# The opening of a one-core hybrid decoder layer: order of the first loads, norms and splits

## The chip, the cores and the metric

The kernel runs on one core of one Trainium2 chip. The metric is the device time of one execution in microseconds; runs of a kernel are given as their median. A profile is one execution, recorded instruction by instruction. Its engines are TensorE (PE, with its weight loads as PEld), VectorE (DVE), ScalarE (ACT), GpSimd (POOL) and SyncE (SP), which here only issues transfers.

## What is computed

One layer of a hybrid decoder over 512 tokens of width 1024, all in float32:

```
u    = RMSNorm(x) * attn_pre_norm
proj = u @ w_in             # delta-rule q, k, v, gate, beta, decay; attention q, k, v
mix  = concat(gated delta rule(proj), block attention(proj)) @ w_out
h    = x + RMSNorm(mix)
h    = h + RMSNorm(relu(RMSNorm(h) @ w_up)^2 @ w_down)
out  = h + sigmoid(h @ w_ple_gate) * (p @ w_ple)
```

The opening, where the change lies, computes `p @ w_ple` (the embedding, 512 x 256 by 256 x 1024), which is stored to memory (`ple`) and read at the very end, the first RMSNorm and its transposes, and the operands of the first projection.

## The kernel before

PE multiplies in a form (fp32r) that takes one pass; to keep float32 accuracy each operand is split into a high and a low half, and each product is three matmuls (`mm3`, L182 for the first, L185 for the others). A split is a cast on ACT (high) and a subtraction on DVE (low): `part_of` (L223, L224) in the embedding, `load_w` (L160, L161) for weights that are loaded into one of three `raw` buffers, and `put_split` (L197, L198) behind the transposes.

The opening is, in the program's order: loads of p, of w_ple's four quarters (on ACT's queue), of x's first 128 tokens and of the identity; a tile `warm` of zeros (memset on DVE) and three products of zeros on PE (L131); a one-column Square on ACT (L132), the first that needs ACT's table, in place on `warm`; the splits of p and w_ple; `embed(0)`, 24 matmuls of 512 columns for the first 512 columns of the embedding, with four copies out of PSUM and their stores; the splits of the other half of w_ple; the load of the norm's weights `nw0` (128 rows of 4 KB, L243, on ACT's queue); the loads and splits of wv in four quarters, with x's other tiles among them; small constants. Then, for each of four tiles of 128 tokens: a Square with its sum on ACT (L258), the inverse root on POOL (`rsqrt`, L148 and L149), the scaling on DVE (L261), eight transposes on PE (L206), and the split of their result into `uT`. `embed(1)` stands behind the first tile. Then come the wv products, 192 matmuls of 260 columns.

No engine's order is written by hand. A planner takes the program's order as ranks, reckons when each instruction's inputs are there, and from it fixes an order for each engine when the kernel is built. On the chip each engine and each transfer queue follows that order, and waits where an input is late. Names with the same tag share a fixed number of buffers: a new tile waits until an old one was read for the last time. The transfers of SP's and ACT's queues count on eight semaphores in turn.

Of the kernel before, what the change touches and what calls it, by code (L numbers as in the profile page):

```python
# [9 lines left out]
F32 = mybir.dt.float32  # L10
F32R = mybir.dt.float32r
AF = mybir.ActivationFunctionType
# [3 lines left out]
P = 128  # L16
T = 512
NT = T // P
D = 1024
# [49 lines left out]
def hybrid_layer(ctx: ExitStack, tc: tile.TileContext, x, p, w_in, w_tok, w_out, w_up, w_down, w_ple, w_gate,  # L69
                 norms, small, consts, rot, out):  # L70
    nc = tc.nc
    PS = bass.MemoryType.PSUM
    cp = ctx.enter_context(tc.tile_pool(name="cp", bufs=1))
    act = ctx.enter_context(tc.tile_pool(name="act", bufs=1))
    phA = ExitStack()
    wp = phA.enter_context(tc.tile_pool(name="wp", bufs=1, side="right"))
# [18 lines left out]
    def pany(name):  # L95
        turn_no[0] += 1
        return (pmm, plv, pmo)[turn_no[0] % 3](name)
# [14 lines left out]
    kc = actB.tile([P, K_END - P], F32, name="kc")  # L112
    sm = cp.tile([P, 57], F32, name="sm")
    nw0 = e.tile([P, D], F32, name="nw0")
    x_h = [e.tile([P, D], F32, tag="x", bufs=4, name=f"x{t}") for t in range(NT)]
    load_x = lambda t: nc.sync.dma_start(x_h[t], x[t * P:(t + 1) * P, :])
# [6 lines left out]
    nc.sync.dma_start(ident, consts[:, K_ID:K_ID + P])  # L123
    for k in range(2):
        nc.scalar.dma_start(wl_in[:, k, 512:D], w_ple[k * P:(k + 1) * P, 512:D])

    warm = e.tile([P, 512], F32, name="warm")
    nc.vector.memset(warm, 0.0)
    pw = ps.tile([P, 512], F32, tag="tr", bufs=2, name="pwarm")
    for _ in range(3):  # L130
        nc.tensor.matmul(pw, warm[:, :P], warm, start=True, stop=True)  # L131
    nc.scalar.activation(warm[:, 0:1], warm[:, 0:1], AF.Square)  # L132

    kcol = lambda c: kc[:, c - P:c]
    tri, ones, neg, ngt = (kcol(c) for c in (K_TRI, K_ONE, K_NEG, K_NGT))
# [10 lines left out]
    def rsqrt(dst, ss, scale, n, eps=EPS):  # L146

        nc.gpsimd.tensor_scalar(dst, ss, scale, eps, op0=ALU.mult, op1=ALU.add)  # L148
        nc.gpsimd.tensor_tensor(dst, dst, half[:, :n], op=ALU.pow)  # L149


    def load_w(src, k0, nk, cols, name):
        n = nk * cols
        raw = wp.tile([P, 1040], F32, tag="raw", bufs=3, name=f"{name}_r")
        hi = wp.tile([P, 1040], F32R, tag="hi", bufs=4, name=f"{name}_h")
        lo = wp.tile([P, 1040], F32R, tag="lo", bufs=4, name=f"{name}_l")

        nc.sync.dma_start(raw[:, :n].rearrange("p (k c) -> p k c", k=nk),
                          src if len(src.shape) == 3 else src[k0 * P:(k0 + nk) * P, :].rearrange("(k p) c -> p k c", p=P))
        nc.scalar.copy(hi[:, :n], raw[:, :n])  # L160
        nc.vector.tensor_sub(lo[:, :n], raw[:, :n], hi[:, :n].bitcast(F32))  # L161
        return (hi[:, :n].rearrange("p (k c) -> p k c", k=nk), lo[:, :n].rearrange("p (k c) -> p k c", k=nk))

    def load_chunk(src, cols, name, nk=KT):

        per = min(nk, 1024 // cols if cols <= 512 else 2)
        got = []
        for k0 in range(0, nk, per):
            hi, lo = load_w(src, k0, per, cols, f"{name}_{k0}")
            got += [(hi[:, i, :], lo[:, i, :]) for i in range(per)]  # L170
        return got

    def load_rows(src, name, order):
        got = {}
        for k0 in order:
            hi, lo = load_w(src, k0, 2, 512, f"{name}_{k0}")
            for i in range(2):
                got[k0 + i] = (hi[:, i, :], lo[:, i, :])
        return got

    def mm3(dst, l, r, start, stop, w_right=False):
        nc.tensor.matmul(dst, l[0], r[0], start=start, stop=False)  # L182
        ops = [(l[0], r[1]), (l[1], r[0])]
        for i, (a, b) in enumerate(ops[::-1] if w_right else ops):
            nc.tensor.matmul(dst, a, b, start=False, stop=stop and i == 1)  # L185
# [14 lines left out]
    def transpose_in(u, dst, t, name):  # L200

        for q in range(2):
            pt = ptr(f"{name}{t}_{q}")
            for i in range(4):
                k = 4 * q + i
                nc.tensor.transpose(pt[:, i * P:(i + 1) * P], u[:, k * P:(k + 1) * P], ident)  # L206
            s = (slice(None), slice(4 * q, 4 * q + 4), slice(t * P, (t + 1) * P))
            put_split((dst[0][s], dst[1][s]), j4(pt))
# [6 lines left out]
    tk = lambda t: slice(t * P, (t + 1) * P)  # L215
    ple = dr.tile([2, T, 512], F32, name="ple")
# [5 lines left out]
    def part_of(both, src, s):  # L222
        nc.scalar.copy(both[0][s], src[s])  # L223
        nc.vector.tensor_sub(both[1][s], src[s], both[0][s].bitcast(F32))  # L224
# [5 lines left out]
    def embed(i):  # L230
        pts = [pany(f"pl{i}_{t}") for t in range(NT)]
        for k in range(2):
            for t in range(NT):
                mm3(pts[t], (pT[0][:, k, tk(t)], pT[1][:, k, tk(t)]), (wl[0][:, k, hf(i)], wl[1][:, k, hf(i)]),
                    k == 0, k == 1, True)
        for t in range(NT):
            s = e.tile([P, 512], F32, tag="pl", bufs=8, name=f"pls{i}_{t}")
            (nc.vector.tensor_copy if t == 3 else nc.scalar.copy)(s, pts[t])
            nc.sync.dma_start(ple[i, tk(t), :], s)
    embed(0)  # L240
    for k in range(2):
        part_of(wl, wl_in, (slice(None), k, slice(512, D)))
    nc.scalar.dma_start(nw0, norms[0:1, :].to_broadcast([P, D]))  # L243
    wv = []
    for t in range(NT):
        wv += load_chunk(w_tok[t * 256:(t + 1) * 256, :], 520, f"wv{t}", nk=2)
        if t == 0:
            load_x(1)
        if t == 1:
            load_x(2)  # L250
            load_x(3)
    nc.sync.dma_start(sm, small)
    nc.sync.dma_start(kc, consts[:, P:])

    for t in range(NT):
        ss = e.tile([P, 1], F32, tag="s1", bufs=4, name=f"ss{t}")
        u = e.tile([P, D], F32, tag="u", bufs=2, name=f"u{t}")
        nc.scalar.activation(u, x_h[t], AF.Square, accum_out=ss)  # L258
        r = e.tile([P, 1], F32, tag="r1", bufs=4, name=f"r{t}")
        rsqrt(r, ss, 1.0 / D, 1)  # L260
        nc.vector.scalar_tensor_tensor(u, x_h[t], r, nw0, op0=ALU.mult, op1=ALU.mult)  # L261
        transpose_in(u, uT, t, "ut")
        if t == 0:
            embed(1)
    ph1.close()
    g = ph2.enter_context(tc.tile_pool(name="g", bufs=1, reuse_waits="tile"))

# [5 lines left out]
    for t0 in (0, 2):  # L273
        pts = {(t, a): pany(f"wv{t}_{a}") for t in (t0, t0 + 1) for a in (0, 260)}
# [155 lines left out]
    for i in (1, 0):  # L430
        for b in range(4):
            s = slice(b * BLK, (b + 1) * BLK)
# [261 lines left out]
    pts = [pany(f"po0{t}") for t in range(NT)]  # L694
# [102 lines left out]
    for g in range(NS):  # L797
        f = F[g % 2]
# [103 lines left out]
    for i in range(2):  # L902
        sr.give(*(s for p_ in wd_s[4 * i:4 * i + 4] for s in p_))
        wg = [x_ for k0 in range(0, KT, 2) for x_ in halves(load_split(w_gate[:, hf(i)], k0))]
        for t in range(NT):
            for c0, c1 in ((0, 512),) if (i, t) != (1, NT - 1) else ((0, 256), (256, 512)):
                n = c1 - c0
                cs = slice(i * 512 + c0, i * 512 + c1)
                sl = take()
                pl, s = sl[:, 0:512], sl[:, 512:D]  # L910
# [54 lines left out]
```

## Time and profile before

| | |
|---|---|
| runs, median (lowest to highest) | 699.1 us (697.05 to 699.86), n = 3 |
| the profiled execution, its own time | 700.27 us |
| its span, first to last instruction | 698.4 us |
| mean granted clock of PE | 0.996 of 2.4 GHz |
| busy: PE, PEld, DVE, ACT, POOL | 682.5, 564.8, 439.0, 324.5, 48.6 us |

The span leaves out some 1.9 us around the instructions. A busy time is a sum over the whole span; an engine whose share is near 1 leaves little for the others to win, and what a stage is worth is read from the wait that ends last in it. Matmul ends are modelled, so two matmuls in a row overlap in the rows and their starts tell the pace.

### The profile page before, as it was taken

To read this page: it belongs to the slowest core of one execution; us is meant where nothing else is said; L and a number is where in the kernel's file an instruction comes from. 1 tells how busy PE (TensorE), PEld (TensorE's weight loads), DVE (VectorE), ACT (ScalarE), POOL (GpSimd) and SP (SyncE) were. 2 spreads that over 40 slices of the span, in tenths; PEclk is the share of its full clock that TensorE was granted. 3 is DMA by queue.
4 is the path that set the end of the run, shared out by engine and by line. 5 is a ranking of instruction groups with operands and counts; after the bars stand their busy time and mean duration, and the time that the engine had idled before them with its cause. 6 is when DMAs were issued, how large, how long until landed. Compare 5 with 4: busy or idle time off the path is not lost. (4 is left out here: it accounts for less than half of the span.)

```text
span 698.4 us, 9002 instructions
## 1 busy us (share of the span) xinstructions
PE 682.5 (98%) x3418; PEld 564.8 (81%) x3418; DVE 439.0 (63%) x687; ACT 324.5 (46%) x598; POOL 48.6 (7%) x91
## 2 busy tenths in 40 slices
PE   8999999999999999999999999999999999999897
PEld 5998888888877768789888888888888888678786
DVE  4748889367676655675386456955778756634532
ACT  6536343433466655445265644454335454523311
POOL 1401100000011100230000000000000000032100
PEclk9999999999999999999999999999999999999999
DMA  8732323532102028286004440154211124544421
GB/s 331 301 122 61 101 86 105 114 109 92 31 31 61 31 61 309 112 258 255 31 31 150 122 150 31 61 151 151 90 35 56 61 76 136 184 84 121 122 77 47
DMA packets 38556, 79.24 MB, mean 113 GB/s; under 512 B 9776, under 2 KB 10416, under 8 KB 38512
## 3 DMA queue, kind: packets, MB, share of 16 engines
q1 hardware_dynamic: 36640, 74.98, 32.7%
q0 software_dynamic: 1152, 2.10, 1.9%
q10 hardware_dynamic: 720, 1.57, 0.6%
q8 instruction: 27, 0.44, 0.3%
q14 instruction: 17, 0.14, 0.1%
HBM read 70.51 MB, written 7.08 MB: 111 GB/s over the span
## 5 line engine op out<-in xcount | busy, mean ns | idle before, releaser
L185 PE MATMUL pd<-sr,sr 128*128 128x512 f32 x464 | 143.6, 390 | 0.6 <-DVE sr L676 0.5
L185 PE MATMUL pu<-u2Tl,sr 128*128 128x512 f32 (+1 forms) x288 | 105.4, 366 | 0.7 <-DVE u2Tl L198 0.7
L182 PE MATMUL pu<-u2Th,sr 128*128 128x512 f32 (+1 forms) x288 | 105.4, 366 | 0.0
L185 PE MATMUL pu<-u2Th,sr 128*128 128x512 f32 (+1 forms) x288 | 105.2, 365 | 0.0
L185 PEld LDWEIGHTS pd<-sr,sr 128*128 128x128 f32 x464 | 86.9, 188 | 19.8 <-DVE sr L676 1.7
L182 PE MATMUL pd<-sr,sr 128*128 128x512 f32 x232 | 90.7, 391 | 0.5 <-ACT sr L675 0.5
L676 DVE TENSOR_TENSOR sr<-sf,sr 128x1024 fp32r<-128x1024 f32 x48 | 58.6, 1222 | 38.5 <-ACT sr L675 14.9
L676 DVE TENSOR_TENSOR sr<-wd,sr 128x1024 fp32r<-128x1024 f32 x42 | 51.3, 1222 | 29.6 <-PE pu L185 28.1
L770 ACT ACTIVATE f<-pu 128x512 f32<-128x512 f32 (+1 forms) x36 | 19.9, 552 | 95.7 <-PE pu L185 95.7
L675 ACT CAST sr<-sf 128x1024 fp32r<-128x1024 f32 x48 | 50.3, 1047 | 27.3 <-DMA sf<-in_w_ple_gate 11.9
L185 PEld LDWEIGHTS pu<-u2Tl,sr 128*128 128x128 f32 x288 | 54.3, 189 | 9.7 <-DVE u2Tl L198 0.9
L185 PEld LDWEIGHTS pu<-u2Th,sr 128*128 128x128 f32 x288 | 54.3, 189 | 8.8
L182 PEld LDWEIGHTS pu<-u2Th,sr 128*128 128x128 f32 x288 | 54.3, 189 | 8.6
L675 ACT CAST sr<-wd 128x1024 fp32r<-128x1024 f32 x42 | 44.2, 1051 | 19.4 <-PE pd L185 19.4
L182 PEld LDWEIGHTS pd<-sr,sr 128*128 128x128 f32 x232 | 43.6, 188 | 10.1 <-ACT sr L675 1.4
L182 PE MATMUL pc<-uTh,w_h 128*128 128x512 f32 x96 | 39.3, 409 | 0.0
L185 PE MATMUL pc<-uTh,w_l 128*128 128x512 f32 x96 | 38.6, 402 | 0.0
L185 PE MATMUL pc<-uTl,w_h 128*128 128x512 f32 x96 | 38.5, 401 | 0.0
L825 DVE TENSOR_TENSOR sf<-sf,pd 128x512 f32<-128x512 f32 x28 | 19.1, 685 | 22.2 <-PE pd L185 22.2
L830 DVE TENSOR_TENSOR wd<-wd,wd 128x1024 f32<-128x1024 f32 x24 | 29.3, 1223 | 0.6
L182 PE MATMUL pg<-sr,h2Th 128*128 128x512 f32 (+1 forms) x72 | 27.2, 377 | 0.0
L185 PE MATMUL pg<-sr,h2Th 128*128 128x512 f32 (+1 forms) x72 | 27.0, 376 | 0.0
(421 smaller groups left out, 1324.2 us busy)
## 6 DMA issues: line engine op xcount, KB each, us to landing
sf<-in_w_up SPq DMA_DIRECT2D x32, 512.0 KB, 3.3
wd<-in_w_down SPq DMA_DIRECT2D x24, 512.0 KB, 4.7
w_r<-in_w_in SPq DMA_DIRECT2D x12, 512.0 KB, 3.6
wo_r<-in_w_out SPq DMA_DIRECT2D x8, 512.0 KB, 3.7
sf<-in_w_ple_gate SPq DMA_DIRECT2D x8, 512.0 KB, 4.3
sf<-in_w_down SPq DMA_DIRECT2D x8, 512.0 KB, 4.3
wv_r<-in_w_tok SPq DMA_DIRECT2D x4, 520.0 KB, 6.6
x<-in_x SPq DMA_DIRECT2D x4, 512.0 KB, 6.9
```

The costliest lines, as they stand in the source:

```text
L182: nc.tensor.matmul(dst, l[0], r[0], start=start, stop=False)
L185: nc.tensor.matmul(dst, a, b, start=False, stop=stop and i == 1)
L675: nc.scalar.copy(hi, src)
L676: nc.vector.tensor_sub(lo, src, hi.bitcast(F32))
L770: nc.scalar.activation(fq[:, side, c0:c1], pt[:, :n], AF.Relu)
L825: add(dst, dst, pts[j])
L830: sub(B[dst + (kk,)], B[x_ + (kk,)], B[y_ + (kk,)])
```

## The change

- The norm's weights `nw0` are loaded on ACT's queue right after w_ple, and x's second tile on SP's right after the identity.
- Two products of zeros instead of three.
- The one-column Square works on a tile of its own, `first`, which POOL sets to zero.
- `load_w` is cut into `load_raw` (the transfer) and `split_raw` (the cast and the subtraction). wv's first three quarters are loaded before x's third and fourth tile; the fourth after the first is split.
- The embedding's copies alternate between ACT and DVE (before: the fourth on DVE); its stores are issued in one row behind the small constants.
- Ranks: norm 0, `embed(1)`, norm 1, the split of wv's first quarter, loads and stores, the splits of the second and third quarter, norm 2, the split of the fourth, norm 3. Before, all wv splits came ahead of all norms.

```diff
--- before.py
+++ after.py
@@ -123,13 +123,17 @@
     nc.sync.dma_start(ident, consts[:, K_ID:K_ID + P])
     for k in range(2):
         nc.scalar.dma_start(wl_in[:, k, 512:D], w_ple[k * P:(k + 1) * P, 512:D])
+    nc.scalar.dma_start(nw0, norms[0:1, :].to_broadcast([P, D]))
+    load_x(1)
 
     warm = e.tile([P, 512], F32, name="warm")
     nc.vector.memset(warm, 0.0)
     pw = ps.tile([P, 512], F32, tag="tr", bufs=2, name="pwarm")
-    for _ in range(3):
+    for _ in range(2):
         nc.tensor.matmul(pw, warm[:, :P], warm, start=True, stop=True)
-    nc.scalar.activation(warm[:, 0:1], warm[:, 0:1], AF.Square)
+    first = cp.tile([P, 1], F32, name="first")
+    nc.gpsimd.memset(first, 0.0)
+    nc.scalar.activation(first, first, AF.Square)
 
     kcol = lambda c: kc[:, c - P:c]
     tri, ones, neg, ngt = (kcol(c) for c in (K_TRI, K_ONE, K_NEG, K_NGT))
@@ -149,17 +153,23 @@
         nc.gpsimd.tensor_tensor(dst, dst, half[:, :n], op=ALU.pow)
 
 
-    def load_w(src, k0, nk, cols, name):
+    def load_raw(src, k0, nk, cols, name):
+        raw = wp.tile([P, 1040], F32, tag="raw", bufs=3, name=f"{name}_r")
+
+        nc.sync.dma_start(raw[:, :nk * cols].rearrange("p (k c) -> p k c", k=nk),
+                          src if len(src.shape) == 3 else src[k0 * P:(k0 + nk) * P, :].rearrange("(k p) c -> p k c", p=P))
+        return raw
+
+    def split_raw(raw, nk, cols, name):
         n = nk * cols
-        raw = wp.tile([P, 1040], F32, tag="raw", bufs=3, name=f"{name}_r")
         hi = wp.tile([P, 1040], F32R, tag="hi", bufs=4, name=f"{name}_h")
         lo = wp.tile([P, 1040], F32R, tag="lo", bufs=4, name=f"{name}_l")
-
-        nc.sync.dma_start(raw[:, :n].rearrange("p (k c) -> p k c", k=nk),
-                          src if len(src.shape) == 3 else src[k0 * P:(k0 + nk) * P, :].rearrange("(k p) c -> p k c", p=P))
         nc.scalar.copy(hi[:, :n], raw[:, :n])
         nc.vector.tensor_sub(lo[:, :n], raw[:, :n], hi[:, :n].bitcast(F32))
         return (hi[:, :n].rearrange("p (k c) -> p k c", k=nk), lo[:, :n].rearrange("p (k c) -> p k c", k=nk))
+
+    def load_w(src, k0, nk, cols, name):
+        return split_raw(load_raw(src, k0, nk, cols, name), nk, cols, name)
 
     def load_chunk(src, cols, name, nk=KT):
 
@@ -235,24 +245,17 @@
                     k == 0, k == 1, True)
         for t in range(NT):
             s = e.tile([P, 512], F32, tag="pl", bufs=8, name=f"pls{i}_{t}")
-            (nc.vector.tensor_copy if t == 3 else nc.scalar.copy)(s, pts[t])
-            nc.sync.dma_start(ple[i, tk(t), :], s)
+            (nc.scalar.copy, nc.vector.tensor_copy)[t % 2](s, pts[t])
+            pls.append((i, t, s))
+    pls = []
     embed(0)
     for k in range(2):
         part_of(wl, wl_in, (slice(None), k, slice(512, D)))
-    nc.scalar.dma_start(nw0, norms[0:1, :].to_broadcast([P, D]))
-    wv = []
-    for t in range(NT):
-        wv += load_chunk(w_tok[t * 256:(t + 1) * 256, :], 520, f"wv{t}", nk=2)
-        if t == 0:
-            load_x(1)
-        if t == 1:
-            load_x(2)
-            load_x(3)
-    nc.sync.dma_start(sm, small)
-    nc.sync.dma_start(kc, consts[:, P:])
-
-    for t in range(NT):
+    raw_v = [load_raw(w_tok, 2 * i, 2, 520, f"wv{i}") for i in range(3)]
+    load_x(2)
+    load_x(3)
+
+    def norm_in(t):
         ss = e.tile([P, 1], F32, tag="s1", bufs=4, name=f"ss{t}")
         u = e.tile([P, D], F32, tag="u", bufs=2, name=f"u{t}")
         nc.scalar.activation(u, x_h[t], AF.Square, accum_out=ss)
@@ -260,8 +263,25 @@
         rsqrt(r, ss, 1.0 / D, 1)
         nc.vector.scalar_tensor_tensor(u, x_h[t], r, nw0, op0=ALU.mult, op1=ALU.mult)
         transpose_in(u, uT, t, "ut")
-        if t == 0:
-            embed(1)
+    wv = []
+
+    def split_v(i):
+        hi, lo = split_raw(raw_v[i], 2, 520, f"wv{i}")
+        wv.extend((hi[:, j, :], lo[:, j, :]) for j in range(2))
+    norm_in(0)
+    embed(1)
+    norm_in(1)
+    split_v(0)
+    raw_v.append(load_raw(w_tok, 6, 2, 520, "wv3"))
+    nc.sync.dma_start(sm, small)
+    nc.sync.dma_start(kc, consts[:, P:])
+    for i, t, s in pls:
+        nc.sync.dma_start(ple[i, tk(t), :], s)
+    for i in (1, 2):
+        split_v(i)
+    norm_in(2)
+    split_v(3)
+    norm_in(3)
     ph1.close()
     g = ph2.enter_context(tc.tile_pool(name="g", bufs=1, reuse_waits="tile"))
```

## Rows read from the trace of the kernel before

**Rows 1.** The page, its first line and part 1.
```profile
span 698.4 us, 9002 instructions
...
PE 682.5 (98%) x3418; PEld 564.8 (81%) x3418; DVE 439.0 (63%) x687; ACT 324.5 (46%) x598; POOL 48.6 (7%) x91
```

**Rows 2.** Waits of PE, whole run: total us, times, longest us.
```profile
PE ut L206 <- DVE u L261: 0.9, 1, 0.9
...
PE ut L206 <- DVE uTl L198: 0.6, 2, 0.4
```

**Rows 3.** Timeline, PE and weight loads (PEld): start us, length us.
```profile
1.44 5.49 PE L131 MATMUL pwarm<-warm 128*128 128x512 f32 x6 [1.44 <-DVE warm L128]
...
4.17 0.34 PEld L131 LDWEIGHTS pwarm<-warm 128*128 128x128 f32 x1 [0.52 <-issue]
...
5.02 0.34 PEld L131 LDWEIGHTS pwarm<-warm 128*128 128x128 f32 x1 [0.52 <-issue]
...
6.73 0.34 PEld L185 LDWEIGHTS pl<-wlh,pTl 128*128 128x128 f32 x1 [0.52 <-issue]
...
7.16 0.45 PE L185 MATMUL pl<-wlh,pTl 128*128 128x512 f32 x1
...
7.45 0.40 PE L182 MATMUL pl<-wlh,pTh 128*128 128x512 f32 x1
...
7.68 0.39 PE L185 MATMUL pl<-wlh,pTl 128*128 128x512 f32 x1
```

**Rows 4.** Timeline, ACT and its queue, the opening.
```profile
2.62 1.28 ACT L223 ACT_TABLE_LOAD   x1 [2.62 <-issue]
4.09 0.62 ACT L223 CAST pTh<-p_in 128x512 fp32r<-128x512 f32 x1 [0.19 <-DMA p_in<-in_p]
4.62 0.61 ACT L223 CAST wlh<-wl_in 128x512 fp32r<-128x512 f32 x1
6.97 0.20 ACT L132 ACTIVATE warm<-warm 128x1 f32<-128x1 f32 x1 [1.74 <-PE pwarm L131]
7.08 0.60 ACT L223 CAST pTh<-p_in 128x512 fp32r<-128x512 f32 x1
...
9.54 0.62 ACT L223 CAST wlh<-wl_in 128x512 fp32r<-128x512 f32 x1 [0.24 <-DMA wl_in<-in_w_ple]
9.55 0.33 ACTq L243 DMA_DIRECT2D nw<-in_norms  x1
...
14.41 1.05 ACT L258 ACTIVATE u<-x 128x1024 f32<-128x1024 f32 x1
```

**Rows 5.** Timeline, SP's queue, the opening.
```profile
0.73 0.85 SPq L120 DMA_DIRECT2D p_in<-in_p  x2
...
2.10 0.43 SPq L123 DMA_DIRECT2D ident<-in_consts  x1
4.26 0.38 SPq L158 DMA_DIRECT2D wv_r<-in_w_tok  x1
```

**Rows 6.** Landing times: nw0's issue (median), and L121's (min/median/max).
```profile
nw<-in_norms ACTq DMA_DIRECT2D x1, 512.0 KB, 6.6
...
DMA to landing us min/median/max: 3.5/4.4/5.3
```

**Rows 7.** Windows: us, busy (x) of PE, PEld, DVE, ACT, POOL; PEclk, DMA, GB/s.
```profile
7.30:10.70 3.40, 3.40 (x17) 2.80 (x16) 2.49 (x4) 2.24 (x5) 0.00 (x0) 1.00 1.06 405
...
655.00:658.70 3.70, 1.64 (x10) 0.96 (x8) 1.69 (x3) 1.18 (x2) 0.00 (x0) 1.00 0.80 168
658.70:662.60 3.90, 3.90 (x13) 3.12 (x14) 0.98 (x2) 0.59 (x1) 0.00 (x0) 0.57 0.66 192
```

**Rows 8.** Timeline, all engines, around the first norm.
```profile
15.91 0.56 POOL L149 TENSOR_TENSOR r<-r,half 128x1 f32<-128x1 f32 x1
...
16.51 1.28 DVE L261 SCALAR_TENSOR_TENSOR u<-x,r,nw 128x1024 f32<-128x1024 f32 x1 [0.73 <-DMA ple<-pls]
...
17.85 1.09 PE L206 MATMUL ut<-ident,u 128*128 128x128 f32 x8 [0.94 <-DVE u L261]
```

## The prediction

> **What bounds the kernel now.** I read the page's first part, then who TensorE (PE) waited for over the whole run, then the opening engine by engine in order of time. PE is busy 682.5 of 698.4 us [rows 1], and what is left is scattered: of its waits the largest that belong to the opening are 1.4 us before the first product of zeros [rows 3], 0.9 us for u, and 0.6 us (two waits) for the low half of uT [rows 2]. The kernel is bound by PE's work, so the opening is worth what it shifts PE's real work, and everything behind moves with it. The most that can be won is small: the three products of zeros and the waits for u and uT. Against a median of 699.1 us, 0.5% is 3.5 us; the three timed runs lie 2.8 us apart, so less than about that can't be told from no change.
>
> In PE's rows the reader should see steps, since the ends are modelled. The weight loads of the zero products stand 0.85 us apart (4.17, 5.02); there are six, two to a product, the first (counted back) at 1.61, so a product takes 1.71 us and the third ends at 6.73, where the second weight load of the embedding appears [rows 3]. The first two matmuls of the embedding are 0.43 us apart (6.73 to 7.16), later ones 0.23 (7.45 to 7.68): 512 columns at 1.2 and at 2.4 GHz. So the clock rose at about 7.3 us, 5.7 us after the first product began, with PE busy all that time [rows 3].
>
> ACT's rows tell why the embedding could not have waited less. After its four transfer issues ACT loads its table (1.28 us), makes the first high halves at 4.09 and 4.62, and is then stuck until 6.97, because the one-column Square writes the tile that the zero products read; the second half's splits start at 7.08 [rows 4].
>
> **The change part by part.**
>
> *One product less.* The zero products end at 1.61 + 4 x 0.855 = 5.03 instead of 6.73: 1.71 us taken off PE. It is a gain only if the embedding's first operands are there. With the splits where they are now (second cast ends at 4.62 + 0.61 = 5.23 [rows 4]) PE could start at about 5.3.
>
> *The table tile of its own.* The Square no longer waits for PE, so the 1.74 us stall of ACT goes [rows 4]. The new memset is one column on POOL, idle then; POOL's work on norms comes far later [rows 8]. By itself this pulls the second half's splits from 7.08 to about 6.3. PE needs them only after the first 12 matmuls, so it is worth nothing as long as those 12 last longer.
>
> *nw0 on ACT's queue, ahead of the Square and of all splits.* This is the part I think decides. Before, eight transfers are issued at once, four by each queue. SP's last of them is at 2.10; its next one, free of any data dependence, is issued only at 4.26 [rows 5], which is when the first transfer of all has landed (the first issues are at 0.73 [rows 5], the quickest landing takes 3.5 us [rows 6]). So the ninth transfer waits for the first. After the change nw0 follows the four w_ple loads on ACT, and it and x1 are the ninth and tenth. A wait at the head of ACT's queue holds everything behind it on ACT: table load, Square, all six splits; DVE waits for those splits, and PE for both.
>
> Where the planner puts nw0 is not certain. In the trace it deviates from the program's order only for what is not ready: the old Square (program order ahead of the splits) stands behind two of them, and nw0 stands where the program has it, behind the last split [rows 4]. An issue that is ready by the planner's reckoning goes by its place in the program. I take it that nw0 stands right behind the w_ple loads, and the first ACT instruction that needs a table, now the Square, behind nw0.
>
> Then: nw0 waits until 4.26, its issue takes 0.33 to 0.45 us (0.33 for nw0 before [rows 4], 0.43 for SP's issues [rows 5]), so 4.66; table load 1.28, so 5.94; Square, and the first cast 0.11 behind its start as at 6.97 and 7.08, so about 6.1; the second cast 0.53 later, ending at 7.2. PE starts the embedding at about 7.3 instead of 6.73. It has stood idle from 5.03, some 2.3 us.
>
> What a table load costs is weighed once more. Its row is 1.28 us, and the cast behind it started 0.19 us after it ended, with its data just landed [rows 4]. The Trainium skill (ScalarE: Activation LUTs, What ACT_TABLE_LOAD costs) adds a drain of 1.38 us to a load of 1.28. By that the splits would begin 1.4 us later still and PE at 8.7; the trace can't rule out a part of it, since nothing was ready sooner, but a cast 0.19 us behind the load excludes the whole, so I go by the row.
>
> *The clock.* Before, it rose with PE busy from 1.6 to 7.3. With a 2.3 us hole in that stretch I expect it to rise later. Near the end, a stretch of 3.7 us in which PE was busy for 1.64 was followed by one at a mean of 0.57 of full speed, that is, mostly at 1.2 GHz [rows 7]. Bounds, counted in embedding matmuls (0.427 us at 1.2, 0.227 at 2.4): if the clock rises at 7.3 all the same, PE has done by then 1.3 or so fewer, or 0.33 us. If it takes the same 5.66 us from the restart, it rises at 12.96: until then 5.66 / 0.427 = 13.3 matmuls, where before 1.2 + 5.70 / 0.227 = 26.3 were done; 13.1 fewer, or 2.97 us. If it stays low for as long as in that late stretch (a mean of 0.57 over 3.9 us is 3.35 us at half speed), 8.3 fewer, or 1.9 us. I take 2.4, midway between the two latter.
>
> The Trainium skill (TensorE: Matmul & The Clock Gate, What's actually happening) says that the low clock is the default and that only activity releases it. This trace agrees for the start (zero products at half speed). It is the rule that speaks against dropping a product when nothing is ready to take its place.
>
> *Norms ahead of wv's splits, nw0 and x1 early.* Now u of the first tile starts at 16.51, right behind the rsqrt on POOL (15.91 + 0.56 = 16.47), and that hangs on ACT's Square at 14.41, which stood behind a wv split; nw0 landed at 9.55 + 6.6 = 16.15 [rows 4, 6, 8]. So nw0 alone would have won only 0.3 us: ranking the norms is the larger half. After: the last w_ple quarter lands at about 9.5 as now [rows 4]; x1 and nw0, 0.5 MiB each, share 405 GB/s [rows 7] and land near 12.1. ACT squares x0 at about 10.2 (behind the last split), r is there by 12.3, u takes 1.28 us [rows 8], so PE can transpose from 13.6 instead of 17.85. At that time PE is still in the embedding, which lasts until 17 now and to about 19 then: the 0.94 us wait goes. The 0.6 us of waits for uT are for space that the DVE halves free; I take half of them gone. Together -1.2 us (bounds 0 and -1.5 [rows 2]).
>
> *The rest.* wv's loads ahead of x2 and x3: x2 and x3 land one or two transfers later (0.5 MiB at 405 GB/s is 1.3 us each [rows 7]); wv's last quarter waits for a free raw buffer. The ple stores go behind wv's last load, sm and kc: their readers come at the very end, so nothing waits. One more of four ple copies on DVE, under PE's embedding work. Each is covered by PE's own work at that time, embedding or wv products, which in the trace waits only for what is named above [rows 2]; without that cover a late tile or split would cost about a load, 1.3 us. Bounds 0 and +1.
>
> **Sum**: +2.4 (late and cold start) -1.2 (waits for u and uT) = +1.2 us. The profiled execution took 700.27 us, 1.2 above the median of the runs; the sum on the median is 700.3.
>
> **Rivals.**
>
> *A. The Square and table load slip ahead of nw0's wait* (the planner counts nw0 as not ready until a transfer lands, and takes what is). For it: ACT would be idle there, and the planner did move the old Square past what was ready. Against: nw0's own place before. The casts start at 4.1 to 4.7, PE at 5.3 to 5.9, its hole is 0.3 to 0.9 us, and if the clock rises at 7.3 as now PE is 0.4 to 0.75 us ahead by then. With the waits, -0.6 - 1.2 = about -1.8: 697.3 us. If the hole costs the rise after all, about -0.2.
>
> *B. The change of the norms gains nothing*: PE's queue has the first transposes at a fixed place, and if that is planned ahead of the second embedding, PE stalls for u at some 12 to 13.6. Worth +1.2 against my sum, 701.5 us. Against it: the cold start delays PE to about 15 before it gets there.
>
> *C. Slower beyond doubt: the clock stays low well past 13 us.* Each further us at 1.2 GHz costs about half a us. From +1.2 with the rise at about 11.8, +3.5 is reached with the rise at about 16.4. The late stretch, back up after 3.4 us, speaks against it; a hole again at the transposes would speak for it. Say 704 us.
>
> **Chances.** My forecast 0.50, A 0.28, B 0.14, C 0.08. The same cases, with the spread of a median of such runs, give faster by over 0.5% 0.04 (A with a downstream order that happens to suit), within 0.5% 0.86, slower 0.10 (C, and the end of B). The range leaves out C and the outer end of A: from A's 697.3, a little under for the spread of runs, to the upper bound 2.97 with nothing recovered, 702.1. So 697.0 to 702.1; the forecast's own range is 699 to 701.5.
>
> **What would show it.** Right: in ACT's rows nw0's issue at about 4.3 and the table load behind it at 4.7, the first cast near 6.1; PE idle from 5.0 to 7.3; steps of 0.43 us in the embedding past 9 us; no wait for u before the first transposes. Wrong: the table load at 2.6 or 3.1 and casts at 4.1 to 4.7 (A); PE waiting for u at 12 (B). The prediction falls as a whole if the planner's order changes further on, where PE's queue has other waits (the score and transposing stages), since a shift of 2 us there is as large as all that I add up.

## The result and the profile after

The changed kernel takes 705.05 us (703.76 to 706.82, 6 runs), the kernel before, run beside it, 699.48 us (697.05 to 701.78, 6 runs): a ratio of 1.0080, 95% interval 1.0056 to 1.0103. It is 5.6 us slower, above the range that was given (697.0 to 702.1).

The page of the changed kernel, first line and part 1, which answers to [rows 1]:

```profile
span 702.2 us, 8998 instructions
...
PE 685.5 (98%) x3416; PEld 563.9 (80%) x3416; DVE 439.2 (63%) x689; ACT 323.1 (46%) x596; POOL 49.6 (7%) x92
```

PE has one product less to do (two of its rows), and is busy 3.0 us longer. A late start would show as idle time; the longer work has another source, of which a low clock in the opening is at most a part. The opening on ACT and its queue, against [rows 4]:

```profile
4.24 0.33 ACTq L126 DMA_DIRECT2D nw<-in_norms  x1
4.61 1.28 ACT L136 ACT_TABLE_LOAD   x1 [4.61 <-DMA wl_in<-in_w_ple]
5.90 0.20 ACT L136 ACTIVATE first<-first 128x1 f32<-128x1 f32 x1
6.01 0.60 ACT L233 CAST pTh<-p_in 128x512 fp32r<-128x512 f32 x1
...
10.25 1.05 ACT L261 ACTIVATE u<-x 128x1024 f32<-128x1024 f32 x1
```

And on PE, against [rows 3]:

```profile
1.45 3.39 PE L133 MATMUL pwarm<-warm 128*128 128x512 f32 x4 [1.45 <-DVE warm L130]
7.18 0.50 PE L192 MATMUL pl<-wlh,pTh 128*128 128x512 f32 x1 [2.34 <-ACT wlh L233]
7.51 0.43 PE L195 MATMUL pl<-wlh,pTl 128*128 128x512 f32 x1
7.75 0.63 PE L192 MATMUL pl<-wlh,pTh 128*128 128x512 f32 x1
8.17 0.63 PE L195 MATMUL pl<-wlh,pTl 128*128 128x512 f32 x1
...
11.16 0.39 PE L195 MATMUL pl<-wlh,pTl 128*128 128x512 f32 x1
11.38 0.39 PE L195 MATMUL pl<-wll,pTh 128*128 128x512 f32 x1
...
14.38 1.03 PE L216 MATMUL ut<-ident,u 128*128 128x128 f32 x8
```

The scaling on DVE, and windows with the granted clock (the third number from the end):

```profile
12.35 1.28 DVE L264 SCALAR_TENSOR_TENSOR u<-x,r,nw 128x1024 f32<-128x1024 f32 x1 [1.29 <-POOL r L153]
```

```profile
5.00:10.00 5.00, 2.82 (x8) 2.27 (x9) 3.19 (x5) 4.05 (x8) 0.00 (x0) 0.77 1.02 382
10.00:15.00 5.00, 5.00 (x24) 4.07 (x23) 3.22 (x4) 4.77 (x9) 2.13 (x4) 0.89 1.04 410
```

The reader sees nw0's issue at 4.24, the table load behind it, the first cast at 6.01, a hole of 2.34 us on PE, a step of 0.24 (7.51 to 7.75), steps of 0.43 us (7.75 to 8.17) that go on until about 11, then steps of 0.22, and the first transposes at 14.38 with no wait. That is nearly the opening that was forecast (where it differs stands below). What it cost is read where it ends, at the first 512-column product of the projection (`pc`): 47.45 us, before 46.62. So 0.8 us of 5.6.

For the rest I laid the two traces side by side, instruction by instruction. From 45 us on every engine has its instructions in the same order in both, and the same PE instruction starts later and later: by 0.8 us at 45 us, 1.8 at 200, 2.8 at 425, 4.8 at 590. (At the end it is 3.8: waits for transfers differ, and the profiled run of before lost time at a low clock near 660 us [rows 7], which that of after did not.) A drift without a new wait is a matter of pace. PE in the middle of the up projection (`pu`), first before, then after:

```profile
429.90 0.39 PE L185 MATMUL pu<-u2Th,sr 128*128 128x512 f32 x1
430.13 0.39 PE L182 MATMUL pu<-u2Th,sr 128*128 128x512 f32 x1
430.36 0.39 PE L185 MATMUL pu<-u2Tl,sr 128*128 128x512 f32 x1
430.58 0.39 PE L185 MATMUL pu<-u2Th,sr 128*128 128x512 f32 x1
```

```profile
433.73 0.40 PE L192 MATMUL pu<-u2Th,sr 128*128 128x512 f32 x1
433.96 0.39 PE L195 MATMUL pu<-u2Tl,sr 128*128 128x512 f32 x1
434.19 0.40 PE L195 MATMUL pu<-u2Th,sr 128*128 128x512 f32 x1
434.43 0.39 PE L192 MATMUL pu<-u2Th,sr 128*128 128x512 f32 x1
```

Three steps take 0.68 us before and 0.70 after. Over the whole trace, of the steps between 222 and 242 ns (512 columns at 2.4 GHz; 226.7 ns is the mean for `pu` before), 498 of 2253 lie over 229 ns before and 1372 of 2260 after. Their sum over 226.7 ns apiece, called the excess below, is 3.3 us before and 9.3 after. Up to 600 us the two differ by 4.35 us; the drift behind the opening is 4.8 - 0.8 = 4.0.

What differs is where the tiles lie. `first` is one column in the pool `cp`, and the built program gives it 32 bytes of each partition; the tiles that are laid out behind it on that side of memory (uT, the second uT, the first eleven weight slabs `sr`) move up by 32, those at the other end stay. Byte address in the partition, and its remainder modulo 256, of what is streamed and of the weights of the same product, in three products of the built programs:

```
                  streamed, mod 256      weights, mod 256
before  pu   44000 224  u2Tl        142816 224  sr (slab 10)
before  pu   27616 224  u2Th        199136 224  sr (slab 11)
before  pd  208864 224  sr          138720 224  sr (slab 9)
after   pu   44032   0  u2Tl        142848   0  sr (slab 10)
after   pu   27648   0  u2Th        199136 224  sr (slab 11)
after   pd  208864 224  sr          138752   0  sr (slab 9)
```

Sorting the steps by whether the streamed address and that of the next product's weights (PEld loads them meanwhile) are equal modulo 256:

```
              before                         after
            steps  mean ns  over 229 ns   steps  mean ns  over 229 ns
equal        1725   227.05       6%        1056   228.19      24%
not equal     481   231.65      74%        1154   233.16      93%
```

Sorted by the product's own weights the shares come out the same (24% and 93% in the changed kernel), so the traces do not tell which of the two counts. Of the 256 slow steps among the equal ones in the changed kernel, 139 stand right behind an unequal step; behind an equal one only 13% are slow.

### The profile page after: what moved, and what is told of

It reads as the page before. It is cut to its first block, busy times and chain, and to the rows that moved or that the text cites. A ratio compares the mean times of both kernels' runs of the same rounds, so it can differ in the third digit from the quotient of the medians.

```text
span 702.2 us, 8998 instructions
## 1 busy us (share of the span) xinstructions
PE 685.5 (98%) x3416; PEld 563.9 (80%) x3416; DVE 439.2 (63%) x689; ACT 323.1 (46%) x596; POOL 49.6 (7%) x92
## 4 chain that ended last, share of the span: by engine, by line
PE 84%; DMA 7%; DVE 3%; ACT 2%; issue 2%; POOL 1%; ACTq 0%; POOLq 0%; DVEq 0%
PE pu L195 16%; PE pd L195 12%; PE pu L192 8%; PE pc L195 6%; PE pd L192 6%; PE pg L195 3%; PE pc L192 3%; PE po L195 3%; PE pmq L195 2%; PE pmk L195 2%; PE wv L195 2%; DMA sf<-in_w_ple_gate 2%; DMA sf<-hd 2%; PE pz L195 2%; PE pg L192 2%
```

## The experiments

The theories: **place** (the 32 bytes make the later products slow, the opening costs 1 to 2 us), and **opening** (the late start and the cold clock cost it all, and what drifts later is chance). In all runs the table gives the median (number of runs), the ratio to the kernel before run beside it with its 95% interval, the excess, and the start of the first `pc`.

| | us (n) | ratio | excess, us | first `pc`, us |
|---|---|---|---|---|
| before (beside the changed kernel) | 699.48 (6) | 1 | 3.3 | 46.6 |
| after | 705.05 (6) | 1.0080 [1.0056, 1.0103] | 9.3 | 47.5 |
| first_in_e | 701.43 (10) | 1.0028 [1.0013, 1.0043] | 3.3 | 48.6 |
| before_pad32 | 704.13 (7) | 1.0066 [1.0040, 1.0091] | 9.2 | 46.5 |
| before_pad128 | 701.37 (10) | 1.0034 [1.0013, 1.0055] | 7.6 | 46.7 |
| before_pad256 | 699.72 (10) | 1.0002 [0.9981, 1.0022] | 3.3 | 47.3 |
| before_aligned | 698.49 (10) | 0.9987 [0.9963, 1.0011] | 1.3 | 46.5 |
| after_three | 704.97 (4) | 1.0066 [1.0048, 1.0084] | 9.2 | 47.2 |
| open_nw_sp | 700.03 (10) | 1.0013 [0.9994, 1.0032] | 3.4 | 48.5 |
| open_aligned | 700.17 (10) | 0.9995 [0.9976, 1.0013] | 1.3 | 48.3 |
| before_two | 701.00 (11) | 1.0003 [0.9987, 1.0020] | 3.3 | 47.3 |
| before_nw_early | 703.81 (5) | 1.0051 [1.0032, 1.0069] | 3.4 | 51.0 |
| open_nw_late | 704.52 (5) | 1.0063 [1.0038, 1.0089] | 3.3 | 51.9 |
| open_mid | 700.27 (12) | 1.0015 [0.9999, 1.0031] | 1.4 | 49.2 |

One caution for the last column: before_pad256 differs from before in no instruction of PE's opening, and its first `pc` starts 0.7 us later (PE waited 1.9 us for u there, not 0.9, and behind that its granted clock was 0.75 from 20 to 25 us, where before it was 1.00). So in the opening less than about 0.7 us may be chance.

### The place of the tiles

**first_in_e**: the changed kernel, the new tile in the opening's own pool, which lies elsewhere.

```diff
-    first = cp.tile([P, 1], F32, name="first")
+    first = e.tile([P, 1], F32, name="first")
```

> The changed kernel, with the tile first taken from the opening's own pool, so that every later tile lies where it lay before; the opening is as in the changed kernel. Theory P (place): most of the loss is that first moves uT, the norm's slabs and all else on the left side by 32 bytes, and a 512-column product goes at 0.233 us instead of 0.227 where streamed operand and next weights no longer lie at equal addresses modulo 256. Then the pace is that of before (some 500 of 2250 steps slow, about 3.3 us over 226.7 ns in all) and only the opening's 0.8 us stays: about 700.3 on a before of 699.5 (699 to 701.5). Rival O (opening: the late and cold start and what follows from it): stays near 705. Rival I (PE's instruction stream is two products shorter and falls differently into its fetches): stays near 705.

The excess is back at 3.3 us and the drift is gone: against before, PE is 2.0 us late from 50 us to 600 us. What is left of the change, a ratio of 1.0028, is its opening.

**before_pad32**, and the same with 32 and 64 columns (**before_pad128**, **before_pad256**): the kernel before with a tile that nothing uses, ahead of the others.

```diff
+    pad = cp.tile([P, 1], F32, name="pad")
+    nc.gpsimd.memset(pad[:, 0:1], 0.0)
     half = cp.tile([P, 16], F32, name="half")
```

> The kernel before, with a one-column tile (32 bytes of each partition) put ahead of the tile half and one POOL memset on it; nothing else. Theory P: all of the loss of pace without the change of the opening: some 1400 slow steps of 2250, about 9.3 us over 226.7 ns, 6 us more than before: about 705 (704 to 706.5). Rivals O and I: no change, 699.5 within 1.

> The kernel before, with a tile of 64 columns (256 bytes) at the same place. Theory P with the period of 256 bytes that the two traces show: no change of pace (500 slow steps), 699.5 within 1. A rival form of P (any move of the left side against the right, or a boundary of 512 or 1024 bytes) would give slow steps and up to 6 us more. Rivals O and I: no change.

> The kernel before with 128 bytes ahead of the tile half. Theory P with a period of 256 bytes: 1133 pairs unequal instead of 578, but unequal by 128 where they were equal, and those are slow in 8 of 10 cases in the two traces: 5 us over before, about 703.5 to 705. With a period of 128 or 64 bytes: no change, 699.5.

The opening of before, untouched, and yet 4.6 us slower with 32 bytes (1.0066), and nothing with 256. PE in `pu` in the two kernels, 32 bytes first:

```profile
429.71 0.39 PE L187 MATMUL pu<-u2Th,sr 128*128 128x512 f32 x1
429.95 0.40 PE L184 MATMUL pu<-u2Th,sr 128*128 128x512 f32 x1
430.18 0.39 PE L187 MATMUL pu<-u2Tl,sr 128*128 128x512 f32 x1
430.41 0.40 PE L187 MATMUL pu<-u2Th,sr 128*128 128x512 f32 x1
```

```profile
429.65 0.39 PE L187 MATMUL pu<-u2Th,sr 128*128 128x512 f32 x1
429.88 0.39 PE L184 MATMUL pu<-u2Th,sr 128*128 128x512 f32 x1
430.11 0.39 PE L187 MATMUL pu<-u2Tl,sr 128*128 128x512 f32 x1
430.33 0.39 PE L187 MATMUL pu<-u2Th,sr 128*128 128x512 f32 x1
```

That is the place theory without any of the opening. With 128 bytes the excess is 7.6 us, so the pattern repeats at 256 and not at 128 or less; the time was lower than I had expected: of 4.3 us more excess some 1.9 us (0.9 to 3.8) came out as time, and why no more isn't shown.

**before_aligned**: the kernel before with the halves of the weights and a scratch tile resized and a small tile put in, so that all 2352 pairs of 512-column products are equal modulo 256 (before 1774).

```diff
-        hi = wp.tile([P, 1040], F32R, tag="hi", bufs=4, name=f"{name}_h")
-        lo = wp.tile([P, 1040], F32R, tag="lo", bufs=4, name=f"{name}_l")
+        hi = wp.tile([P, 1088], F32R, tag="hi", bufs=4, name=f"{name}_h")
+        lo = wp.tile([P, 1088], F32R, tag="lo", bufs=4, name=f"{name}_l")
...
+    apad = actB.tile([P, 16], F32, name="apad")
+    nc.gpsimd.memset(apad[:, 0:1], 0.0)
...
-        jk = m_.tile([P, 512], F32, tag="njk", bufs=1, name=f"{name}j")
+        jk = m_.tile([P, 512], mybir.dt.bfloat16, tag="njk", bufs=1, name=f"{name}j")
```

> The kernel before, with the high and low halves of split weights 1088 columns wide instead of 1040 (256 bytes divide the step from one to the next), 64 bytes put into the pool of the mixing operands, and the Square's unread output in bf16 to make room. All 2352 pairs of streamed operand and next weights then lie at equal addresses modulo 256, where 1774 do in the kernel before. Theory P: the 500 slow steps go, the sum over 226.7 ns falls from 3.3 us to under 0.5, and the time by some 3: 696.5 (695.5 to 697.5). Rival (the slow steps of the projections come from something else, such as the split's traffic on the same memory): 699.5 within 1.

Half right: the excess falls to 1.3 us, not to nothing (the steps of `pc` still have a mean of 228.6 ns), and PE is 2.4 us ahead of before at 600 us in the trace, 3.0 at 640; but the ratio, 0.9987, can't be told from 1.

### The parts of the opening

**after_three**: the changed kernel with the third product of zeros back.

```diff
-    for _ in range(2):
+    for _ in range(3):
```

> The changed kernel with three products of zeros again. Rival I: the instruction stream is as long as before, so the pace comes back: about 699 to 700. Theory P: the tiles lie as in the changed kernel, so the pace stays slow (1400 steps, 9.3 us) and the time near 705; PE is busy to 6.7 and starts the embedding at 7.2 as in the changed kernel, the clock staying up if the hole of 0.5 us lets it: 0.5 to 1.5 us less than the changed kernel, 703.5 to 705. Rival O in the form 'the hole of 2.3 us costs it all': near 700.

PE in its opening:

```profile
1.44 5.49 PE L133 MATMUL pwarm<-warm 128*128 128x512 f32 x6 [1.44 <-DVE warm L130]
7.34 0.53 PE L192 MATMUL pl<-wlh,pTh 128*128 128x512 f32 x1 [0.41 <-ACT wlh L233]
7.70 0.39 PE L195 MATMUL pl<-wlh,pTl 128*128 128x512 f32 x1
7.93 0.39 PE L192 MATMUL pl<-wlh,pTh 128*128 128x512 f32 x1
```

A hole of 0.41 us, and steps of 0.23 us from the second on: the slow steps of the changed kernel came of the long hole, and that of the missing product. Yet the first `pc` starts only 0.24 us sooner than in the changed kernel. Its transposes begin at 13.36, 1.0 us sooner, and its wait for uT ahead of wv's products is longer (1.5 us for 0.8). What the cold clock cost was won back there, and the total is still at 1.0066.

**before_two**: the kernel before with two products and the one-column Square on its own tile (in pool `e`), no more.

```diff
-    for _ in range(3):
+    for _ in range(2):
...
-    nc.scalar.activation(warm[:, 0:1], warm[:, 0:1], AF.Square)
+    first = e.tile([P, 1], F32, name="first")
+    nc.gpsimd.memset(first, 0.0)
+    nc.scalar.activation(first, first, AF.Square)
```

> The kernel before with two products of zeros and the one-column Square on a tile of its own, set to zero by POOL, taken from the pool e, where it moves no operand. Theory (a product less is worth something only where the operands are ready, and the place of the operands is what made the changed kernel slow): ACT's table load stays at 2.6 to 3.1 us and the first casts at 4.1 to 4.7, the embedding starts at 5.1 to 5.9 instead of 5.94, the clock rises where it did (7.3 to 7.8), the first projection starts 0 to 0.6 us sooner than before (46.0 to 46.6), and the excess of the 512-column products over 226.7 ns stays near 3.3 us: 698.8 to 699.8 us. Rival (the hole in front of the embedding keeps the clock low, whatever ACT does): the clock rises 2 us or more later than in the kernel before, steps of 0.43 us go on past 9 us, the first projection starts 1 us or more later, 700.5 us or more.

Both theories missed. The embedding starts at 5.39 us with a hole of 0.16, and with it the clock rises to 2.4 GHz: the steps are 0.23 us from the second on, and the second product starts at 5.76, before at 7.16 [rows 3]. These 1.4 us are lost at the next wait, for u:

```profile
5.39 0.53 PE L184 MATMUL pl<-wlh,pTh 128*128 128x512 f32 x1 [0.16 <-ACT wlh L225]
17.98 1.09 PE L208 MATMUL ut<-ident,u 128*128 128x128 f32 x8 [2.50 <-DVE u L263]
```

The transposes stand where they stood [rows 8], since u is no sooner, and behind that wait the granted clock is 0.74 between 20 and 25 us, as in before_pad256 behind its 1.9 us. Total: 1.0003.

**before_nw_early**: the kernel before, with one line moved.

```diff
         nc.scalar.dma_start(wl_in[:, k, 512:D], w_ple[k * P:(k + 1) * P, 512:D])
+    nc.scalar.dma_start(nw0, norms[0:1, :].to_broadcast([P, D]))
...
-    nc.scalar.dma_start(nw0, norms[0:1, :].to_broadcast([P, D]))
```

> The kernel before with one line moved: nw0's load on ACT's queue right behind the four loads of w_ple. Theory (a ninth transfer at the head of ACT's queue holds ACT until the first transfer has landed): the issue at 4.2 us, the table load at 4.6 instead of 2.6, the first casts at 5.9 and 6.4 instead of 4.1 and 4.6, and the embedding starts at 7.0 to 7.3, with a hole of only 0.2 to 0.5 us since three products of zeros run until 6.7. So the first projection starts 0.3 to 1.3 us later than before (46.9 to 47.9), the excess stays near 3.3 us, 699.7 to 700.8 us. Rival (the issue is not what holds ACT; the table load is late in the changed kernel because the Square has another place): the table load stays at 2.6 to 3.1, the embedding starts at 5.9, the first projection at 46.6 or sooner, 699.5 us or less.

The mechanism that was expected is there (issue at 4.29, table load at 4.66, embedding at 7.30), but the loss by the first `pc` is 4.4 us, not 0.3 to 1.3. ACT, where wv's splits still stand ahead of the embedding's copies and of the norm:

```profile
4.29 0.33 ACTq L126 DMA_DIRECT2D nw<-in_norms  x1
4.66 1.28 ACT L224 ACT_TABLE_LOAD   x1 [4.66 <-DMA wl_in<-in_w_ple]
...
14.82 1.06 ACT L161 CAST wv_h<-wv_r 128x1040 fp32r<-128x1040 f32 x1 [1.57 <-DMA wv_r<-in_w_tok]
15.79 1.56 ACT L239 COPY pls<-pl 128x512 f32<-128x512 f32 x3
17.22 1.08 ACT L258 ACTIVATE u<-x 128x1024 f32<-128x1024 f32 x1
```

```profile
PE ut L207 <- DVE u L261: 2.6, 1, 2.6
...
PE pl L183 <- ACT pls L239: 2.0, 1, 2.0
```

nw0's 0.5 MiB goes ahead of wv's, so ACT stands in front of splits whose quarters come late, and behind them wait the copies that free PE's banks (2.0 us) and the Square of the norm (17.22, before 14.41 [rows 4]).

**open_nw_late**: the changed kernel with `first` in `e`, and nw0's load back on ACT's queue behind the splits of w_ple.

```diff
-    nc.scalar.dma_start(nw0, norms[0:1, :].to_broadcast([P, D]))
     load_x(1)
...
-    first = cp.tile([P, 1], F32, name="first")
+    first = e.tile([P, 1], F32, name="first")
...
+    nc.scalar.dma_start(nw0, norms[0:1, :].to_broadcast([P, D]))
```

> The changed kernel with its one-column tile in the pool e, and nw0's load back on ACT's queue behind the splits of w_ple; everything else of the change stays. Theory: ACT is free, the table load at 2.6 to 3.3 us, the embedding starts at 5.1 to 5.9 as in the kernel before; but nw0 then lands at some 16 us while the first norm's Square is done at 11, so u is late and PE waits 1.5 to 3 us for it ahead of the first transposes, where the changed kernel waits for nothing; the first projection starts 0.5 to 2 us later than in the kernel before (47.1 to 48.6), the excess stays near 3.3 us, 699.8 to 701.3 us. Rival (nw0's early issue is the only thing in the opening that costs): with it gone the first projection starts 1 us or more sooner than in the kernel before (45.6 or less), 698.5 us or less.

ACT is free early as expected, but the wait for u is twice what I had put down. DVE, and PE's first wait:

```profile
17.53 1.28 DVE L264 SCALAR_TENSOR_TENSOR u<-x,r,nw 128x1024 f32<-128x1024 f32 x1 [5.84 <-DMA nw<-in_norms]
```

```profile
PE ut L215 <- DVE u L264: 5.8, 1, 5.8
```

The granted clock is 0.69 from 15 to 20 us and 0.62 from 20 to 25, and the first `pc` is 5.3 us late. So nw0 early and the norms ranked early lose 4 to 5 us each when done alone, and 1 to 2 together.

**open_nw_sp**: `first` in `e`, nw0 on SP's queue behind x's second tile, so that ACT is free; **open_aligned**: the same with the resized tiles of before_aligned.

```diff
-    nc.scalar.dma_start(nw0, norms[0:1, :].to_broadcast([P, D]))
     load_x(1)
+    nc.sync.dma_start(nw0, norms[0:1, :].to_broadcast([P, D]))
...
```

> The changed kernel with first in the opening's pool (pace of before), and nw0 issued on SP's queue behind x1 instead of on ACT's ahead of the splits. My theory of the opening: the wait at the head of ACT's queue is what made the opening slower; without it the table load comes at 2.6, the casts at 4.1, PE starts the embedding at about 5.3, and the norms still come early: 1 to 2.5 us less than first_in_e (701.4), so 699 to 700.4; ahead of before by up to 1 if no new wait comes. Rival: the opening's loss lies in the order behind the embedding (PE waiting for uT's high half at the first wv products, 1.6 us in first_in_e), which this leaves as it is: 701 as first_in_e.

> open_nw_sp together with before_aligned: the two theories' gains add: some 3 us less than open_nw_sp, 695.5 to 697.5, below both kernels. If either theory is wrong it shows in which of the two singles it lacks.

The embedding starts at 5.35 us, and PE is then at the first transposes by 11.1, where it waits for u:

```profile
PE ut L216 <- DVE u L264: 2.9, 1, 2.9
```

u itself starts at 12.65, only 0.3 us later than in the changed kernel (nw0 lands 0.7 later); in open_aligned the wait is 2.8. The early start is given back whole.

**open_mid**: everything learned in one kernel: nw0's issue on ACT behind the first two casts, the first tile's transposes ranked behind the whole embedding, `first` in `e`, tiles resized as in before_aligned.

```diff
...
         part_of(wl, wl_in, (slice(None), k, slice(0, 512)))
+        if k == 0:
+            nc.scalar.dma_start(nw0, norms[0:1, :].to_broadcast([P, D]))
...
-    norm_in(0)
+    u0 = norm_in(0)
     embed(1)
-    norm_in(1)
+    transpose_in(u0, uT, 0, "ut")
+    transpose_in(norm_in(1), uT, 1, "ut")
```

> A kernel made from what the runs showed: two products of zeros, the table load on a tile of its own in the pool e, nw0 on ACT's queue behind the first two casts (by then the first transfer has landed, so the issue has nothing to wait for), x's second tile early and the norms' Squares and scalings ranked as in the changed kernel, but the first tile's transposes ranked behind the whole embedding; the tiles of the later stages are laid so that streamed operand and next weights are equal modulo 256 bytes, as in before_aligned. Theory (early nw0 and early norms pay only together, and an issue costs nothing once the first transfer has landed): casts at 4.1 to 4.7, nw0's issue at 5.2 to 5.4, the embedding starts at 5.3 to 5.5 and runs to some 17 us without a wait, no wait of PE for u of more than 0.5 us, the first projection starts at 45.8 to 46.5 us (before 46.63), the excess is 1.3 us: 696.5 to 698.5 us, a ratio of 0.995 to 0.999 to the kernel before. Rival 1 (what is won ahead is lost at the next wait, as in every opening tried): a new wait of 1 us or more in front of the transposes or the first wv products, the first projection at 46.8 or later, 698.5 to 700 us. Rival 2 (the clock falls in the stretch of transposes): a mean granted clock under 0.9 somewhere between 15 and 30 us, 1 us or more lost there.

Rival 1 holds, but for a total 0.3 us above its range. The embedding runs from 5.41 to 16.5 us without a wait, and PE then waits for DVE:

```profile
16.53 1.03 PE L215 MATMUL ut<-ident,u 128*128 128x128 f32 x8
18.55 0.51 PE L191 MATMUL wv<-wv_h,uTh 128*128 128x260 f32 x2 [0.99 <-ACT uTh L206]
22.27 0.76 PE L215 MATMUL ut<-ident,u 128*128 128x128 f32 x4 [3.21 <-DVE uTl L207]
```

```profile
16.88 2.39 DVE L167 TENSOR_TENSOR wv_l<-wv_r,wv_h 128x1040 fp32r<-128x1040 f32 x2
19.18 1.28 DVE L249 COPY pls<-pl 128x512 f32<-128x512 f32 x2
20.38 1.23 DVE L167 TENSOR_TENSOR wv_l<-wv_r,wv_h 128x1040 fp32r<-128x1040 f32 x1
21.53 1.28 DVE L207 TENSOR_TENSOR uTl<-ut,uTh 128x512 fp32r<-128x512 f32 x2
```

Splits of wv, copies and halves of uT now all come at once, and the first `pc` starts at 49.2. Rival 2 holds as well; the granted clock behind the wait:

```profile
20.00:25.00 5.00, 2.73 (x15) 2.73 (x16) 4.72 (x7) 2.22 (x5) 1.82 (x2) 0.77 1.01 348
25.00:30.00 5.00, 5.00 (x40) 5.00 (x40) 4.23 (x5) 2.16 (x4) 1.34 (x2) 0.89 1.04 414
```

nw0's issue came at 6.51, not 5.2 to 5.4: in the built program it is the eleventh transfer, behind x's second tile and wv's first quarter, and waited for the third, a quarter of w_ple, to land (6.49). No kernel here is faster than the one before by more than its interval.

## Why the prediction was wrong

**The step that failed** is the cost of the tile of its own, put at "one column on POOL", that is, nothing. No price was set on the place that it takes. It moves later operands by 32 bytes, and their products then take some 233 ns for 227: 3.6 us of the 5.6 (705.05 against 701.43 in first_in_e) to 4.6 (before_pad32). That it is the place is shown by first_in_e (one word changed, excess 9.3 to 3.3) and before_pad32 (nothing changed but 32 bytes, excess 3.3 to 9.2, 4.6 us). Why equal remainders modulo 256 are faster isn't shown; that PE's stream and PEld's load get in each other's way in memory would fit, and no run tells. Nor is the remainder all: 24% of the equal steps in the changed kernel are over 229 ns, over half of them right behind an unequal one, and in before_aligned 8% still are.

**nw0 ahead of ACT's work: right.** Forecast 4.26 for the issue, 4.7 for the table load, 6.1 for the first cast, 7.3 for PE with a hole of 2.3; measured 4.24, 4.61, 6.01, 7.18 and 2.34. Rival A, that the Square slips ahead, did not happen.

**The table load: the row was right.** The Square starts at 5.90, 0.01 us behind the load's end (4.61 + 1.28). The drain of 1.38 us that the Trainium skill (ScalarE: Activation LUTs, What ACT_TABLE_LOAD costs) adds does not show here, nor in the first cast at 6.01.

**The clock: another course, and almost worthless.** The term was set on a rise that comes later, between 7.3 and 12.96. In the trace of the changed kernel the granted clock rises to 2.4 GHz at 4.32 us, under the last zero product and sooner than before (7.26), so the step from 7.51 to 7.75 is a fast one. At 7.73, with PE idle from 4.84 to 7.18, it falls to 1.2 GHz, and at 11.15 it is back. By then PE had started 10 products of the embedding, before 19: 9 fewer, or 2.0 us at 0.227, where 2.4 was taken. The size was near by luck, since the first rise falls anywhere from 5.44 to 7.33 us in the five profiles whose opening is that of the kernel before (before, the three with a pad, before_aligned). The rule cited (TensorE: Matmul & The Clock Gate, What's actually happening, in the Trainium skill), that activity lifts the clock from its low default, agrees in that the slow steps stand behind a hole of 2.3 us here and 2.5 in first_in_e; behind holes of 0.4 us (after_three) and 0.8 (before_nw_early) there are none. But at the first `pc` the cold clock is worth 0.24 us (after_three), no more than chance: PE waits for uT there anyway. The term should have been set against the next wait and not summed.

**The waits for u: gone, but not for the reason given.** u starts at 12.35 and the transposes at 14.38 have no wait; forecast 12.3 and 13.6. PE was in the embedding at 13.6, but only until 14.38 and not to about 19: in its order the first transposes stand behind 24 of the embedding's 48 products, which is the order that rival B feared. What kept B's stall away was the late start, as the prediction says against B: PE comes 0.75 us behind the end of u (13.63). Where PE is early it stalls: 0.3 us in after_three, 2.9 in open_nw_sp. So the -1.2 us is not a price of its own, and hangs on the +2.4. Nor do the parts of the change have prices of their own: before_nw_early and open_nw_late show that nw0 early and the norms early lose 4.4 and 5.3 us by the first `pc` when apart.

**The sum.** For the opening +1.2 was forecast; it is 0.8 in the profile of the changed kernel and 2.0 in first_in_e, whose ratio of 1.0028 is +1.9 us (0.9 to 3.0). The size was right, in part by luck: the late start and the wait for u are two sides of one thing and do not add up. The prediction's last sentence named a changed order further on as what would bring it down; the order did not change, the pace did.

## What to carry to other kernels

A new tile is not free even if nothing waits for it: compare the addresses of the operands before and after, and put small additions where they move none, or make the first rows that you compare the steps of the longest stage, since 1.1% of pace in `pu` (229.25 ns a step for 226.7), and like amounts elsewhere, outweighed the late start here. In an opening whose engines wait on each other, price a change at the next wait behind it, not at the spot: here a start 1.4 us sooner gained nothing (before_two), and two rearrangements that lose 4 to 5 us apart lose 1 to 2 together. A load at the head of an engine's own queue holds all the engine's work while it waits for an earlier transfer.

## What was not expected of the hardware

- A 128x512 product at 2.4 GHz does not have one pace here: most steps take 226 or 227 ns, the others mostly 229 to 237, and which it is goes with the streamed address minus that of the weights (the next product's, or its own) modulo 256: before, 6% of the steps were over 229 ns at a difference of 0, 47% at 64, 78% at 128 and 98% at 192.
- Some of PE's waits in the opening are followed by stretches at 1.2 GHz that cost as much as some of the waits: behind 2.5 us in before_two a granted clock of 0.74 over 5 us, behind 5.8 us in open_nw_late 0.69 and 0.62 over 5 us each. Not all are: behind 2.6 us in before_nw_early it stayed at 1.00.
